# A hybrid decoder step on one Trainium2 core: the first stage reordered, seven up blocks on the first columns, four gates between the layers

## Chip, core and metric

One core of a Trainium2 chip runs the whole step as one launch. The metric is the device time of a launch in microseconds, as the median of several executions. One further execution is taken with the profiler, and its trace is what the rows below come from.

## The reference, cut to what matters

Two layers; 512 prompt rows and 8 sample rows (520 columns in the kernel) share the weights, D = 1024, all in float32.

```python
def block(x, ...):
    m, *states = mixer(rmsnorm(x, n_mix_pre), ...)
    x = x + rmsnorm(m, n_mix_post)
    f = square(relu(rmsnorm(x, n_ffn_pre) @ w_up)) @ w_down      # w_up 1024 x 4096
    return x + rmsnorm(f, n_ffn_post), *states

def mixer(xn, ...):
    rq, rk, rv, rg, hq, hf, hi, hgt, z, xbc, dt, gates = split(xn @ w_in)
    y_r = ...   # retention, 4 heads
    y_h = ...   # HGRN2, 8 heads: f from hf and a lower bound lb, q from hq, v from hi, gate hgt
    y_m = ...   # Mamba-2, 4 groups: conv on xbc, z, dt (16 columns), d_skip
    merged = sum over b of sigmoid(gates[b]) * (y[b] @ w_branch[b])
    return merged @ w_out, new states
```

## The kernel before, in words

**Blocks.** Activations lie transposed: 8 tiles of 128 channels by 520 columns. A projection block is 128 output channels. `mm3` (L210) makes it from three float32r products for each of 8 k-tiles (high weight by high activation, high by low, low by high), each on two column ranges, 0 to 256 and 256 to 520: 48 matmuls into one of two PSUM buffers (`pj`, L237). XN and YB are the two pairs of high and low activations. Called with `halves=(0,)` or `(1,)` it does one range only, 24 matmuls, a half block.

**Weights.** `wload` (L158) loads 512 KB into one of four raw buffers by SP and splits it on ACT (high part, L174) and DVE (low part, L175), four pieces each. The split parts go to two "w" buffers, to two sets of four general "u" tiles, or, for some, to parts of XN or YB. The list of uses is written out by hand from L1219 on; `weights` (L183) takes the next use and starts loads for up to AHEAD = 4 uses later, as long as their kind of buffer has one free.

**Order.** The program is traced in the order of the code, with `step()` moving generators ("tails") on by one yield after each block. A scheduler then orders each engine's queue by priority and its own time estimate: an instruction whose inputs it takes as ready may go earlier than traced. `keep_in_program_order` holds an instruction behind the one traced before it on its engine.

**First stage** (L1266 to 1308). SP loads x and the gain; one weight load is issued ahead (L1278). For five groups of rows ACT squares, DVE adds, POOL takes the power (L1286), DVE scales (L1290), PE transposes, ACT and DVE write XN (L1296, L1297). Then POOL loads the lower-bound logits (`lbr`) and eleven lists of rows in all (`vec_rows`, L376), SP the small ones of `params` (L407: dt_bias, a_log, d_skip, state_conv), the constants `cst` (1387 KB) and the masks. In layer 0 the first two blocks of head 0 are begun on the first columns.

**Between the layers.** The last down projection runs on the first columns, then on the second. `chain` (L335) for each range takes the mean square (`rstd`, L292: PE, DVE, POOL, DVE, PE, ACT), adds the residual, writes the next YB or XN without the norm's factor and at its end makes that factor, RR. Layer 1 begins (L1340 to 1353) with head 0's four blocks on YB's first columns, scaled by RR afterwards (`scaled`, L240). When the second range's chain is done, the tails `spill_x` and `normalized` (XN = norm of x, L368) are started, and head 0 does the second columns of its four blocks from the weights kept for it. Eight HGRN heads follow, each in eight steps; beside them `gate_ahead` (L1100) makes the 16 gates of branches 1 and 2 and stores them in DRAM. The 8 gates of branch 0 come late, after branch 2, into T1 (L1370).

**Up projection.** In the first group (`up_order`, L1199) NUP = 5 blocks run on the first columns while the chain of the second columns runs; then four of them from kept weights and the fifth from reloaded ones on the second; the other three on both. Their results (L1392) need RR.

## Time and profile before

| what | value |
|---|---|
| median of 3 runs | 2787.74 us (2787.11 to 2789.95) |
| the profiled execution, its own time | 2785.26 us |
| its span, first to last instruction | 2783.5 us |
| mean granted TensorE clock | 0.990 |
| PE busy, DVE, ACT, POOL | 98%, 61%, 42%, 26% of the span |

The span is what the rows below are measured in; their times start at its first instruction. Granted clock 1.00 is 2.4 GHz, 0.50 is 1.2 GHz. PE's matmuls are pipelined, so a matmul's own duration (some 283 ns) overlaps the next; the count in a window tells the rate.

### The profile page before, as it was taken

The page shows a single profiled execution, that of the slowest core. Times are in us where ns is not written, and L with a number is a line of the kernel's source. Part 1 is how long each engine was busy: PE and PEld are TensorE (multiplying, and loading weights), DVE is VectorE, ACT ScalarE, POOL GpSimd, SP SyncE. Part 2 cuts the span into 40 slices and gives each one's busy share as a digit, 9 for nine tenths or more (in the row PEclk, how much of TensorE's full clock was granted, in tenths as well). Part 3 has the DMA queues.
Part 4 walks back from the last instruction along what each step waited for, and adds up shares of the span by engine and source line. Part 5 has one row for each costly group of instructions (what it writes and reads, how often), then busy time and mean ns, then how long its engine had stood idle before and what let it go on. Part 6 is the DMA issues. An engine that isn't in the chain of part 4 may idle for free.

```text
span 2783.5 us, 56807 instructions
## 1 busy us (share of the span) xinstructions
PE 2720.9 (98%) x22489; PEld 2638.7 (95%) x22489; DVE 1690.8 (61%) x3714; ACT 1166.0 (42%) x2856; POOL 735.6 (26%) x939
## 2 busy tenths in 40 slices
PE   5999999999999999999989999999999999999999
PEld 5999999999999989999979999999999999899998
DVE  4575759986765553443576665799775645534443
ACT  3354545534333443332445444555253234533333
POOL 2353534341222031000144344434221310300004
PEclk8999999999999999999989999999999999999999
DMA  5544445573554413333324444456644534233331
GB/s 143 140 120 120 116 127 138 148 206 105 150 164 122 145 55 92 95 91 92 107 70 130 124 116 120 123 144 166 182 124 139 172 99 139 59 92 92 92 99 62
DMA packets 607578, 335.37 MB, mean 120 GB/s; under 512 B 96080, under 2 KB 581968, under 8 KB 607184
## 3 DMA queue, kind: packets, MB, share of 16 engines
q1 hardware_dynamic: 606672, 331.59, 42.4%
q8 instruction: 178, 2.92, 0.4%
q14 instruction: 88, 0.72, 0.1%
q0 software_dynamic: 640, 0.15, 0.0%
HBM read 287.61 MB, written 44.06 MB: 119 GB/s over the span
## 4 chain that ended last, share of the span: by engine, by line
PE 89%; DVE 4%; DMA 2%; issue 2%; ACT 2%; POOL 1%; SPq 1%; POOLq 0%; DVEq 0%; ACTq 0%
PE pj L215 78%; PE pm L290 3%; PE pm L506 1%; PE pm L466 1%; PE pm L514 1%; PE pm L882 1%; DVE w L175 1%; DMA wr<-in_w_in_dram 1%; ACT w L174 1%; DVE T L355 1%; PE pm L885 1%; PE pm L1049 0%; PE pm L1018 0%; DVE XL L360 0%; PE pm L633 0%
## 5 line engine op out<-in xcount | busy, mean ns | idle before, releaser
L215 PE MATMUL pj<-XH,w 128*128 128x256 f32 (+2 forms) x8896 | 1506.5, 286 | 7.7 <-ACT XH L282 3.5
L215 PEld LDWEIGHTS pj<-XH,w 128*128 128x128 f32 (+1 forms) x8896 | 1255.5, 188 | 30.7 <-issue 11.1
L174 ACT ACTIVATE w<-wr 128x256 fp32r<-128x256 f32 x1552 | 517.0, 404 | 1109.2 <-PE pj L215 980.3
L215 PE MATMUL pj<-XL,w 128*128 128x256 f32 (+2 forms) x4448 | 941.3, 286 | 5.4 <-DVE XL L360 3.3
L175 DVE TENSOR_TENSOR w<-wr,w 128x256 fp32r<-128x256 f32 x1552 | 651.8, 473 | 377.1 <-ACT w L174 376.8
L215 PEld LDWEIGHTS pj<-XL,w 128*128 128x128 f32 (+1 forms) x4448 | 703.7, 188 | 19.5 <-issue 10.7
L215 PE MATMUL pj<-YH,w 128*128 128x256 f32 (+1 forms) x3456 | 577.4, 285 | 5.3 <-DVE T L1120 2.3
L215 PEld LDWEIGHTS pj<-YH,w 128*128 128x128 f32 x3456 | 489.0, 189 | 11.7 <-ACT w L174 4.7
L215 PE MATMUL pj<-YL,w 128*128 128x256 f32 (+1 forms) x1728 | 366.0, 284 | 1.0 <-DVE YL L360 0.9
L215 PEld LDWEIGHTS pj<-YL,w 128*128 128x128 f32 x1728 | 275.9, 189 | 3.0 <-DVE YL L360 2.3
L320 POOL TENSOR_TENSOR u<-u,u 128x256 f32<-128x256 f32 (+1 forms) x56 | 47.3, 844 | 565.8 <-ACT u L319 565.8
L1392 DVE SCALAR_TENSOR_TENSOR u<-pj,RR 128x520 f32<-128x520 f32 (+2 forms) x74 | 46.1, 625 | 172.1 <-PE pj L215 169.9
L1409 POOL TENSOR_SCALAR T<-T,gn 128x256 f32<-128x256 f32 (+1 forms) x16 | 16.1, 1006 | 298.9 <-ACT u L316 298.9
L1404 DVE TENSOR_TENSOR T<-T,pj 128x520 f32<-128x520 f32 x32 | 22.3, 696 | 115.3 <-PE pj L215 115.3
L949 POOL TENSOR_TENSOR u<-u,cst 128x520 f32<-128x520 f32 x16 | 22.1, 1380 | 201.3 <-ACT u L948 191.3
L290 PE MATMUL pm<-ident,u 128*128 128x128 f32 (+3 forms) x320 | 49.7, 276 | 20.5 <-DVE u L1290 20.4
L628 POOL TENSOR_TENSOR u<-u,s 128x512 f32<-128x512 f32 x32 | 39.1, 1240 | 86.2 <-DMA u<-in_state_hgrn_dram 73.5
L290 PEld LDWEIGHTS pm<-ident,u 128*128 128x128 f32 (+3 forms) x320 | 37.3, 145 | 22.6 <-DVE u L1290 10.9
L290 PE MATMUL pm<-ident,T 128*128 128x128 f32 (+1 forms) x368 | 56.3, 282 | 1.3 <-DVE u L1164 1.0
L1122 POOL TENSOR_TENSOR T<-T,u 128x520 f32<-128x520 f32 x16 | 29.1, 1822 | 99.8 <-DVE u L1120 99.8
L754 POOL TENSOR_TENSOR u<-u,u 128x544 f32<-128x544 f32 x32 | 45.9, 1434 | 34.8 <-DVE u L753 34.8
L863 POOL COPY s<-u 128x4 f32<-128x4 f32 x32 | 17.3, 543 | 142.1 <-ACT u L861 142.1
(319 smaller groups left out, 3346.3 us busy)
## 6 DMA issues: line engine op xcount, KB each, us to landing
wr<-in_w_in_dram SPq DMA_DIRECT2D x208, 512.0 KB
wr<-in_w_up_dram SPq DMA_DIRECT2D x66, 512.0 KB
wr<-in_w_down_dram SPq DMA_DIRECT2D x64, 512.0 KB
u<-rbd SPq DMA_DIRECT2D x96, 256.0 KB
wr<-in_w_branch_dram SPq DMA_DIRECT2D x48, 512.0 KB
out_dram<-u SPq DMA_DIRECT2D x72, 256.0 KB
out_dram<-u SPq DMA_DIRECT2D x72, 128.0 KB
gate<-u SPq DMA_DIRECT2D x32, 260.0 KB
```

The source lines that it names most:

```text
L174: a = S.activation(out=hi, in_=rq, func=AF.Copy)
L175: b = V.tensor_tensor(out=lo, in0=rq, in1=hi.bitcast(F32), op=ALU.subtract)
L215: PE.matmul(ps[:m, CH[h]], lhsT=wt(k), rhs=act[:, k, CH[h]], start=st, stop=sp_)
L290: PE.transpose(out, in_, ident[:k, :k])
L320: (eng or V).tensor_tensor(out=acc, in0=acc, in1=sq, op=ALU.add)
L355: V.tensor_tensor(out=x, in0=x, in1=t, op=ALU.add)
L466: PE.matmul(po[32 * c:32 * c + 32, :2 * width], lhsT=qz[:, c, :], rhs=st[:, off:off + 2 * width], start=True, stop=True, tile_position=(0, ...
L506: PE.matmul(pl[:, cs[c]], lhsT=w[:, cs[c]], rhs=u[:, cs[c]], start=True, stop=True)
L628: G.tensor_tensor(out=c3(sts[i]), in0=c3(sts[i]), in1=bc(fs[:, s0, None], shc), op=ALU.mult)
L754: G.tensor_tensor(out=c, in0=c, in1=e, op=ALU.add)
L1122: G.tensor_tensor(out=T2[:, d, :], in0=T2[:, d, :], in1=dst, op=ALU.add)
L1392: V.scalar_tensor_tensor(out=a, in0=ps[:, c], scalar=0.0, in1=RR[:, c], op0=ALU.max, op1=ALU.mult)
```

## The change

- First stage: the logits' and layer 0's row loads on POOL come ahead of the x loads. Two weight loads are placed after the second and third group of rows, with their splits in traced order. The constants are loaded in two parts, the larger one (K_COS to K_RK, up to K_TRI) only after head 3 of layer 0; dt_bias, a_log, d_skip and state_conv are loaded after head 1 of layer 0 and used after head 3, in layer 1's case after the third and the fourth MLP group of layer 0. d_skip comes as one contiguous broadcast of 16 numbers, and POOL copies out of it.
- The 16-column dt weights: load and split are held in traced order; their block runs on columns 0 to 512 and 512 to 520.
- NUP is 7: seven up blocks on the first columns, then 3 to 6 from kept weights and 0 to 2 from reloaded ones on the second, then block 7 on both.
- Layer 1: after head 0's four first-column blocks, four gates of branch 0 (d = 0 to 3) on the first columns; after the chain the same four on the second, from kept weights, with tanh and a store to DRAM. Head 0's weights are loaded a second time. Late in layer 1 only gates 4 to 7 are left; the branch reads the other four from DRAM. The gates beside the heads are two for each head in both layers.

```diff
@@ -47,7 +47,8 @@
 AHEAD = 4
-NUP = 5
+NUP = 7
+NEG = 4
@@ -152,13 +153,18 @@
 
+    def pin(ins):
+        tc.keep_in_program_order(ins)
+
...
         raw = wp.tile([P, NB, n], F32, tag=f"raw{n}", name=nm("wr"), bufs=4 if n == 128 else 1)
-        SY.dma_start(out=raw, in_=src.rearrange("(k p) m -> p k m", p=P))
+        dma = SY.dma_start(out=raw, in_=src.rearrange("(k p) m -> p k m", p=P))
+        if n != 128:
+            pin(dma)
@@ -173,19 +179,25 @@
             b = V.tensor_tensor(out=lo, in0=rq, in1=hi.bitcast(F32), op=ALU.subtract)
-            if key in pinned:
-                tc.keep_in_program_order(a)
-                tc.keep_in_program_order(b)
+            if key in pinned or n != 128:
+                pin(a)
+                pin(b)
...
 
-    def weights(src, ahead=False):
+    def preload():
+        key = order.pop(0)
+        live[key_info[key][2]] += 1
+        pinned.add(key)
+        wload(key)
+
+    def weights(src):
...
         key = uses[i]
-        assert ahead or key[0] == str(src), i
+        assert key[0] == str(src), i
         for j in list(order):
-            if first[j] > i + (0 if ahead else AHEAD):
+            if first[j] > i + AHEAD:
@@ -195,24 +207,20 @@
             order.remove(j)
-            if ahead:
+            with tc.high_priority(WOFF):
                 wload(j)
-            else:
-                with tc.high_priority(WOFF):
-                    wload(j)
-        if ahead:
-            return
...
 
-    def mm3(ps, w, ah, al, halves=(0, 1), m=P, ks=range(NB)):
+    def mm3(ps, w, ah, al, halves=(0, 1), m=P, ks=range(NB), cuts=None):
...
                 for h in halves:
-                    PE.matmul(ps[:m, CH[h]], lhsT=wt(k), rhs=act[:, k, CH[h]], start=st, stop=sp_)
+                    c = (cuts or CH)[h]
+                    PE.matmul(ps[:m, c], lhsT=wt(k), rhs=act[:, k, c], start=st, stop=sp_)
@@ -248,13 +256,18 @@
             return ps
-        ps = pj()
         if (l, c0) in early:
+            ps = pj()
...
             return raw
-        mm3(ps, weights(w_cols(l, c0, n)), *XN, m=n)
+        if n != P:
+            ps = psj.tile([P, 1024], F32, tag="pj", name=nm("pj"))[:, :T]
+            mm3(ps, weights(w_cols(l, c0, n)), *XN, m=n, cuts=(slice(0, SEQ), slice(SEQ, T)))
+            return ps
+        ps = pj()
+        mm3(ps, weights(w_cols(l, c0, n)), *XN)
@@ -412,18 +425,6 @@
             vec_rows(rb, 8 * i, a[l])
-        sc = pp.tile([16, 4], F32, tag="sc", name=nm("sc"))
-        SY.dma_start(out=sc[:, 0:1], in_=dt_bias[l].rearrange("(h o) -> h o", o=1))
-        SY.dma_start(out=sc[:, 1:2], in_=a_log[l].rearrange("(h o) -> h o", o=1))
-        dk = pp.tile([P, 8], F32, tag="dk", name=nm("dk"))
-        dv = d_skip[l].rearrange("(b two) -> two b", two=2)
-        for q in range(2):
-            SY.dma_start(out=dk[64 * q:64 * q + 64, :], in_=dv[q:q + 1, :].to_broadcast([64, 8]))
-        rcs = []
-        for hf in range(4):
-            rc = ut()[:24, :512]
-            SY.dma_start(out=rc, in_=state_conv[l].rearrange("s r c -> (s r) c")[:, 512 * hf:512 * hf + 512])
-            rcs.append(rc)
@@ -442,8 +443,24 @@
         p["lb"] = lbp
+        yield
+        sc = pp.tile([16, 4], F32, tag="sc", name=nm("sc"))
+        pin(SY.dma_start(out=sc[:, 0:1], in_=dt_bias[l].rearrange("(h o) -> h o", o=1)))
+        pin(SY.dma_start(out=sc[:, 1:2], in_=a_log[l].rearrange("(h o) -> h o", o=1)))
+        dk = pp.tile([P, 8], F32, tag="dk", name=nm("dk"))
+        dv = sp.tile([P, 16], F32, tag="dv", name=nm("dv"), bufs=1)
+        pin(SY.dma_start(out=dv, in_=d_skip[l:l + 1, :].to_broadcast([P, 16])))
+        rcs = []
+        for hf in range(4):
+            rc = ut()[:24, :512]
+            pin(SY.dma_start(out=rc, in_=state_conv[l].rearrange("s r c -> (s r) c")[:, 512 * hf:512 * hf + 512]))
+            rcs.append(rc)
+        yield
...
         p["sc"] = sc
+        for q in range(2):
+            x = slice(64 * q, 64 * q + 64)
+            G.tensor_copy(out=dk[x, :], in_=dv[x, :].rearrange("p (b two) -> p b two", two=2)[:, :, q])
@@ -1093,15 +1110,24 @@
     def gates_at(l, h, i):
-        at = {0: (3,), 1: (0, 1, 3)}.get(h, (1, 3)) if l else (1, 3)
-        n = 2 * h - (l > 0 and h == 1)
-        return [(1 + g // NB, g % NB) for g in (n + k for k, x in enumerate(at) if x == i)]
+        return [(1 + g // NB, g % NB) for g in (2 * h + i // 2,) if i % 2]
+
+    early_gates = [(0, d) for d in range(NEG)]
+
+    def late_from(l):
+        return NEG if l else 0
+
+    def g_col(b, d):
+        return C_GATE + 1024 * b + 128 * d
...
     def gate_ahead(l, b, d):
-        ps = proj(l, C_GATE + 1024 * b + 128 * d)
+        ps = proj(l, g_col(b, d))
...
         S.activation(out=t, in_=ps, func=AF.Tanh, scale=0.5)
-        gates[l, b, d] = kept = dp.tile([P, T], F32, tag="gate", name=nm("gate"), bufs=2 * NB)
+        keep_gate(l, b, d, t)
+
+    def keep_gate(l, b, d, t):
+        gates[l, b, d] = kept = dp.tile([P, T], F32, tag="gate", name=nm("gate"), bufs=2 * NB + NEG)
@@ -1109,7 +1135,7 @@
         for d in range(NB):
-            if mode == "last":
+            if mode == "last" and d >= late_from(l):
@@ -1218,8 +1244,15 @@
         held = {}
-        for i, c in enumerate(early_cols if l else early_cols[:2]):
-            held[c] = add(w_cols(l, c), store="wu"[i % 2] if l else "w")
+        if l:
+            for i, c in enumerate(early_cols):
+                add(w_cols(l, c), store="wu"[i % 2])
+            gheld = [add(w_cols(l, g_col(*g)), store="wu"[i % 2]) for i, g in enumerate(early_gates)]
+            for key in gheld:
+                use(key)
+        else:
+            for c in early_cols[:2]:
+                held[c] = add(w_cols(l, c))
@@ -1239,7 +1272,7 @@
             add(w_br(l, 2, d))
-        for d in range(NB):
+        for d in range(late_from(l), NB):
@@ -1265,6 +1298,11 @@
     xts = [[t[:, :512], t[:, 512:]] for t in xts] + [xs_]
+    lbr = sp.tile([P, P], F32, tag="prow", name="lbr", bufs=3)
+    for j in range(depth):
+        vec_rows(lbr, 8 * j, hg_lb_logits[j])
+    loading = params(0, prms[0])
+    next(loading)
@@ -1274,7 +1312,6 @@
         SY.dma_start(out=xs_[i], in_=rows[4][0][:, 512 * i:512 * i + 512])
-    weights(None, True)
@@ -1295,17 +1332,14 @@
             V.tensor_tensor(out=lo, in0=c3(ps)[:, :, :n], in1=hi.bitcast(F32), op=ALU.subtract)
-    lbr = sp.tile([P, P], F32, tag="prow", name="lbr", bufs=3)
-    for j in range(depth):
-        vec_rows(lbr, 8 * j, hg_lb_logits[j])
-    loading = params(0, prms[0])
-    next(loading)
-    SY.dma_start(out=cst, in_=cst_in)
+        if c in (1, 2):
+            preload()
+    pin(SY.dma_start(out=cst[:, K_TRI:], in_=cst_in[:, K_TRI:]))
     mskf = uw(384)
-    SY.dma_start(out=mskf, in_=msk_in)
+    pin(SY.dma_start(out=mskf, in_=msk_in))
...
     lba = lower_bounds(lbr)
-    next(loading, None)
+    next(loading)
@@ -1338,17 +1372,23 @@
         else:
-            spare = [T2[:, i, :] for i in (0, 2, 7, 1)]
-            for i, c in enumerate(early_cols):
-                raw = spare[i]
+            spare = [T2[:, i, :] for i in (0, 2, 7, 1, 3, 4, 5, 6)]
+            for raw, c in zip(spare, early_cols + [g_col(*g) for g in early_gates]):
...
                 scaled(raw, ps, 0)
-                early[(l, c)] = raw
                 step()
+            early.update(((l, c), raw) for c, raw in zip(early_cols, spare))
...
             tails.append(normalized(XN, p["mpre"]))
+            for raw, g in zip(spare[len(early_cols):], early_gates):
+                ps = pj()
+                mm3(ps, weights(w_cols(l, g_col(*g))), *YB, halves=(1,))
+                scaled(raw, ps, 1)
+                S.activation(out=raw, in_=raw, func=AF.Tanh, scale=0.5)
+                keep_gate(l, *g, raw)
+                step()
@@ -1356,6 +1396,11 @@
                 G.memset(RR, 0.0)
+            if l == 0 and h == 1:
+                next(loading)
+            if l == 0 and h == 3:
+                next(loading, None)
+                pin(SY.dma_start(out=cst[:, :K_TRI], in_=cst_in[:, :K_TRI]))
@@ -1367,7 +1412,7 @@
             split((YB[0][:, d, :], YB[1][:, d, :]), T1[:, d, :])
-        for d in range(NB):
+        for d in range(late_from(l), NB):
@@ -1419,6 +1464,9 @@
             if gi == 2 and l + 1 < depth:
+                next(loading)
+                next(loading)
+            if gi == 3 and l + 1 < depth:
```

## Rows read from the trace of the kernel before

**Rows 1.** The page, parts 1 and 2: PE's total; granted clock in 40 slices, in tenths.
```profile
PE 2720.9 (98%) x22489; PEld 2638.7 (95%) x22489; DVE 1690.8 (61%) x3714; ACT 1166.0 (42%) x2856; POOL 735.6 (26%) x939
...
PEclk8999999999999999999989999999999999999999
```

**Rows 2.** Windows of 20 us: stretch, length, busy us (instructions) of each engine, clock, DMA.
```profile
1020.00:1040.00 20.00, 17.94 (x146) 16.68 (x144) 14.44 (x22) 8.95 (x21) 8.76 (x9) 1.00 0.10 28
1040.00:1060.00 20.00, 17.53 (x125) 16.57 (x124) 6.67 (x19) 8.33 (x23) 6.74 (x10) 0.83 0.26 77
1240.00:1260.00 20.00, 20.00 (x169) 20.00 (x168) 10.61 (x24) 9.53 (x23) 0.00 (x0) 1.00 0.28 80
1400.00:1420.00 20.00, 18.15 (x139) 16.48 (x138) 14.27 (x31) 5.75 (x15) 5.73 (x6) 0.92 0.33 107
1420.00:1440.00 20.00, 15.10 (x96) 13.75 (x94) 15.18 (x30) 11.52 (x23) 9.72 (x14) 0.82 0.23 80
1440.00:1460.00 20.00, 16.53 (x129) 15.85 (x130) 16.23 (x25) 7.37 (x15) 13.39 (x13) 0.83 0.21 54
...
2400.00:2420.00 20.00, 16.41 (x110) 14.69 (x109) 12.64 (x22) 9.44 (x23) 8.92 (x9) 0.84 0.09 27
```
The five busy columns are PE, PEld (weight load), DVE, ACT and POOL; then granted clock, DMA share, GB/s.

**Rows 3.** Waits of PE, whole span: us in total, times, longest.
```profile
PE pm L290 <- DVE u L1290: 20.4, 3, 9.9
```

**Rows 4.** The chain that ended last, first 60 us: start, us, what.
```profile
16.92 16.28 DMA wr<-in_w_in_dram
...
46.84 6.46 PE pj L215 x34
```

**Rows 5.** Windows of 2 us in the first stage, columns as in rows 2.
```profile
20.00:22.00 2.00, 2.00 (x16) 2.00 (x15) 1.96 (x4) 1.74 (x6) 0.47 (x1) 1.00 0.05 0
...
46.00:48.00 2.00, 1.41 (x6) 1.40 (x7) 0.76 (x5) 0.22 (x1) 1.47 (x3) 0.50 1.03 186
```

**Rows 6.** Timeline of the first stage: start, us, instruction, idle before and its end.
```profile
7.09 0.55 POOL L1286 TENSOR_TENSOR s<-s,nhalf 128x1 f32<-128x1 f32 x1 [5.38 <-DVE s L1285]
...
22.57 0.14 DVE L1284 TENSOR_TENSOR s<-s 8x1 f32<-8x1 f32 x1
...
33.18 11.08 SPq L161 DMA_DIRECT2D wr<-in_w_in_dram  x3
33.22 0.59 ACT L174 ACTIVATE w<-wr 128x32 fp32r<-128x32 f32 x4 [11.15 <-DMA wr<-in_w_in_dram]
...
33.59 0.13 DVE L1285 TENSOR_SCALAR s<-s 8x1 f32<-8x1 f32 x1
...
34.29 1.30 POOL L378 DMA_DIRECT2D lbr<-in_hg_lb_logits_dram  x2
...
36.41 0.81 PE L215 MATMUL pj<-XH,w 128*128 128x264 f32 x2
...
46.53 0.52 POOL L378 DMA_DIRECT2D rb<-in_norm_mix_post_dram  x1 [7.82 <-DMA lbr<-in_hg_lb_logits_dram]
```

**Rows 7.** DMA issues, first 80 us: line, engine, count, KB, us from issue to landing.
```profile
lbr<-in_hg_lb_logits_dram POOLq DMA_DIRECT2D x2, 4.0 KB, 11.7
...
rb<-in_norm_mix_post_dram POOLq DMA_DIRECT2D x1, 4.0 KB, 3.9
```

**Rows 8.** Timeline between the layers: the second range's mean square, 16 matmuls of 2 columns.
```profile
1425.59 1.07 PE L298 MATMUL pm<-ones,u 128*66 128x2 f32 x16
```

**Rows 9.** The page, part 5: the weight splits, busy us, mean ns, idle before.
```profile
L174 ACT ACTIVATE w<-wr 128x256 fp32r<-128x256 f32 x1552 | 517.0, 404 | 1109.2 <-PE pj L215 980.3
...
L175 DVE TENSOR_TENSOR w<-wr,w 128x256 fp32r<-128x256 f32 x1552 | 651.8, 473 | 377.1 <-ACT w L174 376.8
```

**Rows 10.** Instructions by line, 990 to 1060 us: ns min/median/max, first and last start, forms.
```profile
L1392 DVE SCALAR_TENSOR_TENSOR u<-pj,RR x10: 409/424/433, 1018.2 to 1055.2; 128x256 f32<-128x256 f32 x5, 128x264 f32<-128x264 f32 x5
...
L360 DVE SCALAR_TENSOR_TENSOR XL<-T,gn,XH x10: 471/490/1324, 1010.5 to 1038.2; 128x264 fp32r<-128x264 f32 x8, 128x256 fp32r<-128x256 f32 x2
...
L283 POOL TENSOR_TENSOR YL<-u,YH x10: 727/753/907, 1020.9 to 1057.3; 128x256 fp32r<-128x256 f32 x5, 128x264 fp32r<-128x264 f32 x5
```

## The prediction, made before the changed kernel was built

> **What bounds the kernel now.** I read the page's totals first. The reader should see that TensorE (PE) is busy 98% of the span and that its granted clock leaves full speed in only a few of the 40 slices [rows 1]. So the kernel is PE-bound nearly everywhere, and a change that adds no PE work can gain only where PE stands or runs at its lower level.
>
> The table of windows says how much. A dense 20 us window holds 169 matmuls, 0.118 us each, so a half block of 24 matmuls is worth 2.84 us. The three windows of the gap between the layers hold 139, 96 and 129 matmuls instead of 507: 143 are missing, 16.9 us. The two windows around the second pass of the first up group hold 146 and 125 in layer 0 (67 missing, 7.9 us), and 110 in layer 1's worst one (59 missing, 7.0 us) [rows 2]. In these windows the granted clock averages 0.82 to 0.92: PE fell from 2.4 to 1.2 GHz after it had stood for lack of input.
>
> The first stage is the biggest hole. In the list of PE's waits its transposes stand 20.4 us for the normalized rows (L1290) [rows 3]. The chain of waits then names what follows, 16.28 us for a weight load, and at its end 34 matmuls that take 6.46 us, 0.19 us each [rows 4], because the granted clock is at 0.50 by then [rows 5]. They end at 53.30 us. The timeline shows the mechanism. At 22.57 us VectorE (DVE) adds the sums of the last rows. Its next instruction is a split of a 128x32 piece of the 16-column dt weights, which waits for ScalarE (ACT), which waits 11.15 us for the DMA; the sample rows go on only at 33.59 and the second half's first matmul comes at 36.41. PE then meets the transpose of the lower-bound logits, which POOL issued only at 34.29 us, and stands until 46.6, when POOL too is released [rows 6]. The SP queue shows why loads land late: the weight issues from 33.18 on take 11.08 us, right behind the second pair of d_skip loads, and in a 2 us window behind the first pair the DMA engines are 0.05 busy and move nothing [rows 5, 6].
>
> **The change part by part.** The profiled execution took 2785.26 us (span 2783.5); the median of the runs shown, 2787.74, is 2.48 above it. I make the sum against the first and add 2.48.
>
> *First stage.* Three things go: the early dt split, the logits behind the row work, and the element-by-element d_skip load. After 22.57 the sample rows need the 2.82 us that [rows 6] show from 33.59 to 36.41, so the second half could begin at 25.5. What is late next is POOL: the eleven row loads are now pinned ahead of its first power, which ran at 7.09. Eleven issues at 0.52 to 0.65 us end near 7.5, and the ninth waits for the first to land, as it did before (7.82 us) [rows 6]. Landing took 11.7 us behind the d_skip loads and 3.9 us for the last three [rows 7]; I take a value near the 3.9, since nothing clogs the queue now. That delays the first 128 rows by 0 to 2.5 us, partly hidden under the second; I put 1 us and start at 26.5. The 36 matmuls that had been done at 53.30 then need 36 x 0.118 = 4.2 us, and the state of 53.30 is reached at 30.7: 22.6 us gained. The bounds are 24 (no delay) and 11 (one of the two waits stays). The weights of the next blocks were landing in 26 to 50 us before; now the DMA has no silence, so I charge nothing. If that cover is gone, each late load holds PE for about a half block, 2.8 us.
>
> *Small loads moved.* dt_bias, a_log, d_skip, state_conv and the large part of the constants are issued on SP later, in traced order, some behind stores that wait for compute. Weight loads queue behind them, but four raw buffers hold 20 us of PE work. Two POOL copies per layer and the transposes of the conv state move, not grow. The dt weights are split in traced order, so ACT may stand for their landing again; PE has two PSUM blocks, 11.4 us, before it notices. I charge 1 us in all, with 0 to 5 per layer as bounds.
>
> *dt block.* 48 matmuls of 256 and 264 columns become 24 of 512 and 24 of 8. The trace has none of 8; 16 of 2 columns took 1.07 us, 0.07 each [rows 8]. With 24 x 0.22 (estimated as just under twice 0.118) + 24 x 0.07 = 6.9 against 5.7, I charge 1.2 us per layer, 2.4 in all; bounds 0 and 2 per layer.
>
> *Seven up blocks.* Two more half blocks (5.7 us) run before PE needs the second half of XN, and two weights more are loaded per layer. A load costs ACT 4 x 0.33 and DVE 4 x 0.42 = 1.68 us [rows 9]. So DVE gets two splits and two evictions at 0.42, 4.2 us, in the stretch in which it also runs the chain whose end (RR of the second half) releases PE by way of the evictions (L1392) [rows 10]. DVE was busy 14.44 of the 20 us from 1020 [rows 2], so I let half of the 4.2 delay the chain: 5.7 - 2.1 = 3.6 us per layer, 7.2 in all. Bounds are 0 and 5.7 each.
>
> Here a second row speaks against the change: a split of the chain (L360) takes 0.49 us in the median but up to 1.32 [rows 10]; in the timeline the slow ones lie beside POOL's additions (L363). Two more of POOL's subtractions (L283), 0.75 us each, come into this stretch. If each holds DVE for its length, 1.5 us per layer go too. The Trainium skill (GPSIMD Engine Reference, Key points) says the same in general: GpSimd shares its SBUF interfaces with VectorE and contends with its two-input instructions. By that rule the gain would be 2.1 instead of 3.6 per layer.
>
> *Four gates between the layers.* Eight half blocks, 22.7 us of PE work, move from late in layer 1, where PE is dense, into the gap. The layer's later gates lose half their blocks; the remaining four, 22.7 us, still cover the 8 splits of YB before the first branch. New on SP are four stores and four reloads of 260 KB, and four weight loads more, because head 0's weights are no longer kept. DVE, busy 45.7 of the 60 us, gets 8 splits (13.4 us) and 8 evictions (3.4 us): 62.5 us. PE then has 364 x 0.118 + 22.7 = 65.7 us of dense work where it took 60 + 22.7. If nothing stands the gain is 16.9. If DVE keeps the share of its busiest window, 0.81, the stretch takes 77 us and the gain is 5.6. PE also has to live through the RR chain that begins at 1425.59 with two PSUM buffers, and the eight steps of normalizing XN (L325) now run under gates that don't need XN [rows 8]. I take 10, between the ends; the range goes from 3 to 16.9.
>
> Sum: 22.6 + 7.2 + 10 - 2.4 - 1 = 36.4, so 2748.9 profiled and **2751** for the median.
>
> **Rivals.**
> *DVE becomes the bound in the up stretch and in the gap.* For it: its share there and the stretched L360; against it: its free 5.6 us from 1020 on. The up blocks then bring nothing and the gap 4: 22.6 + 4 - 3.4 = 23, so 2765. The Trainium skill's sharing of SBUF interfaces (GPSIMD Engine Reference, Key points) would point this way.
> *Only one of the two waits of the first stage goes,* because POOL's row loads still hold the powers, or a load still lands late. The start brings 11: 2787.7 - (11 + 17.2 - 3.4) = 2763. Against it: the silence of the DMA queue follows the d_skip loads both times.
> *Everything fits:* 24 + 11.4 + 16.9 - 1 = 51, so 2736. Against it: both stretches have a chain that ends in a PE, POOL, DVE, PE, ACT sequence which no block removes.
> *Slower: the dt split.* Place: before head 5, in both layers. ACT stands in order for the 64 KB of 64-byte runs, DVE behind it, and PE once its two buffers are full. The load took 16.28 us on the chain [rows 4], of which some 5 would show per layer. It decides the sign only from a landing of about 32 us, when it costs 21 per layer: 36 gained, 42 lost, 2793. The landing lay behind a silent queue before, which speaks against it.
> *The change does not do what it says:* the scheduler still orders by its own estimate, and the pin holds an instruction only behind its predecessor. That would look like the second rival, and is counted there.
>
> **How the numbers follow.** Forecast 0.53, DVE-bound 0.22, one start wait left 0.08, everything fits 0.12, slower 0.03, and 0.02 for a sum of mishaps that lands on no change. Within 0.2% (5.6 us, about what a measurement of this kernel can tell from none) lies only that last case. The forecast's own range, from the bounds of the three gains taken together, is 2742 to 2760. Taking in the two cases near 2764 and leaving out most of 2736, the range is 2738 to 2768.
>
> **What would show it.** Right: the sample rows' first 264-column matmul near 26 us and the first dense window from about 28; no dt split before 100 us; no silent DMA windows in the first 50 us; matmul counts in the up windows up by some 30 per layer and in the gap's windows above 130 each; four gates with line numbers of the new early loop. Wrong: POOL waiting behind its ninth row load past 12 us; DVE at 19 of 20 us in the gap with PE waiting on it; ACT idle for over 10 us before a 128x32 split; PE waits in the steady stretches that hold none now.

## The result and the profile after

The changed kernel takes **2758.89 us** in the median (2757.0 to 2760.38) against 2787.43 for the kernel before on the same chip: a ratio of 0.9897, interval 0.9882 to 0.9913, so 28.5 us less. The forecast was 2751 with a range of 2738 to 2768: faster as forecast, inside the range, 8 us short of the size. The profiled execution took 2760.38 us (span 2758.4) against 2785.26 (span 2783.5), 24.9 less; the ledger below is made on these two. That is 3.6 us under the difference of the medians, since the profiled execution of the changed kernel is the slowest of its four and that of the kernel before lies under its median.

The page, parts 1 and 2, answers to [rows 1]: PE does the same 22489 matmuls in 12 us less busy time, and no slice's clock lies under nine tenths now.

```profile
PE 2709.0 (98%) x22489; PEld 2625.5 (95%) x22489; DVE 1699.1 (62%) x3754; ACT 1177.2 (43%) x2896; POOL 746.9 (27%) x951
...
PEclk9999999999999999999999999999999999999999
```

The table of 20 us windows answers to [rows 2], with the same columns. The three windows of the gap hold 447 matmuls where they held 364, at full clock. The second window of the up group holds 154 in both layers, where the worst of before held 125 and 110.

```profile
1000.00:1020.00 20.00, 18.19 (x143) 17.47 (x143) 14.11 (x33) 10.91 (x30) 7.42 (x8) 0.95 0.44 125
1020.00:1040.00 20.00, 18.55 (x154) 18.26 (x154) 13.30 (x25) 10.57 (x28) 9.33 (x10) 0.96 0.10 27
1400.00:1420.00 20.00, 17.22 (x143) 16.23 (x142) 15.27 (x33) 7.59 (x20) 4.97 (x4) 1.00 0.48 146
1420.00:1440.00 20.00, 17.43 (x139) 16.88 (x139) 18.73 (x39) 15.03 (x29) 1.32 (x2) 1.00 0.48 141
1440.00:1460.00 20.00, 18.71 (x165) 18.15 (x164) 15.55 (x32) 11.62 (x29) 14.22 (x23) 1.00 0.50 138
...
2380.00:2400.00 20.00, 18.29 (x154) 17.70 (x155) 15.28 (x28) 10.98 (x29) 10.52 (x10) 1.00 0.19 53
```

The list of PE's waits answers to [rows 3]. The wait for the normalized rows fell from 20.4 to 12.8 us; 12.0 of it is the wait for the first rows at the start of the run. The second line is new: PE waits for ScalarE's weight split, twice for over 3 us.

```profile
PE pm L303 <- DVE u L1327: 12.8, 3, 12.0
PE pj L223 <- ACT w L180: 8.5, 4, 3.4
PE pj L223 <- DVE T L249: 3.9, 4, 1.3
PE pj L223 <- DVE u L1437: 3.6, 2, 1.8
```

The timeline of the first stage answers to [rows 6]. POOL's ninth row load waits 2.10 us for the first to land, and the first power runs at 10.57 us (7.09 before). The second column range's matmuls, which began at 36.41, begin at 27.86 and are dense from 29.40.

```profile
7.89 0.52 POOL L391 DMA_DIRECT2D rb<-in_norm_mix_post_dram  x1 [2.10 <-DMA lbr<-in_hg_lb_logits_dram]
...
10.57 0.61 POOL L1323 TENSOR_TENSOR s<-s,nhalf 128x1 f32<-128x1 f32 x1
...
27.86 0.52 PE L223 MATMUL pj<-XH,w 128*128 128x264 f32 x2
...
29.40 0.39 PE L223 MATMUL pj<-XL,w 128*128 128x264 f32 x1 [0.76 <-DVE XL L1334]
```

**The ledger.** Start times of the same instruction in both traces give the lead of a run: how many us earlier than in the kernel before it starts. Heads are the HGRN heads, counted from 0 and taken at one ACT instruction of each (L519 before, L536 now); the dt block lies between heads 4 and 5. Below it stand the leads of the runs of the next section.

```
event (its time before)            changed  x1    x2    x9    x3    x10   x8    x11   x7
head 2, layer 0 (140.1)              20.4  19.9  21.2  20.3  19.9  20.5  17.4  22.6  20.1
head 4, layer 0 (228.0)              19.1  18.6  19.9  19.1  18.7  19.2  16.1  21.4  18.8
head 5, layer 0 (279.4)              12.4  17.1  15.0  17.8  13.0  17.9  15.1  20.3  13.3
first up group begins (968.8)        12.4  17.0  15.1  18.2  13.4  18.0  15.2  20.3  13.4
up group is over (1171.0)            16.0  20.6  18.6  21.3  13.7  16.5  18.6  24.9  16.9
end of layer 0 (1401.4)              17.2  21.8  19.8  22.6  14.9  17.8  19.9  26.2  18.1
head 2, layer 1 (1512.2)              3.6   8.5   6.3   9.3   1.7   4.5   6.3  12.9  15.3
head 7, layer 1 (1739.1)             -2.1   6.2   1.0   8.0  -3.9   2.2   4.9  11.6   9.3
first up group begins (2341.1)       20.7  29.3  23.7  30.6  18.5  25.8  27.3  34.4   9.6
up group is over (2544.4)            25.8  33.7  28.7  34.6  17.2  25.1  32.7  38.9  12.9
end (2780.1)                         25.1  33.1  28.1  34.0  17.2  25.1  32.2  38.3  12.3
```

The first stage gains 20.4, the up groups 3.6 and 5.1, the gap 17.2 to 3.6 and later, when the moved gates are missing, -2.1 to 20.7: -13.6 + 22.8 = 9.2. Against them stand **6.7 and 5.7 us lost at the dt block**, in layer 0 and layer 1.

### The profile page after: what moved, and what is told of

It reads as the page before. It is cut to its first block, busy times and chain, and to the rows that moved or that the text cites. A ratio compares the mean times of both kernels' runs of the same rounds, so it can differ in the third digit from the quotient of the medians.

```text
span 2758.4 us, 56964 instructions
## 1 busy us (share of the span) xinstructions
PE 2709.0 (98%) x22489; PEld 2625.5 (95%) x22489; DVE 1699.1 (62%) x3754; ACT 1177.2 (43%) x2896; POOL 746.9 (27%) x951
## 5 line engine op out<-in xcount | busy, mean ns | idle before, releaser
L223 PE MATMUL pj<-XH,w 128*128 128x256 f32 (+2 forms) x8768 | 1485.9, 286 | 13.3 <-ACT w L180 7.7
L223 PEld LDWEIGHTS pj<-XH,w 128*128 128x128 f32 (+1 forms) x8768 | 1235.8, 188 | 38.6 <-ACT w L180 15.9
L180 ACT ACTIVATE w<-wr 128x256 fp32r<-128x256 f32 x1584 | 528.1, 404 | 1064.6 <-PE pj L223 962.2
L223 PE MATMUL pj<-XL,w 128*128 128x264 f32 (+2 forms) x4384 | 931.4, 286 | 0.8 <-DVE XL L1334 0.8
L181 DVE TENSOR_TENSOR w<-wr,w 128x256 fp32r<-128x256 f32 x1584 | 665.5, 473 | 370.4 <-ACT w L180 369.2
L223 PEld LDWEIGHTS pj<-XL,w 128*128 128x128 f32 (+1 forms) x4384 | 693.8, 188 | 14.6 <-issue 11.3
L223 PE MATMUL pj<-YH,w 128*128 128x256 f32 (+1 forms) x3584 | 597.7, 284 | 8.2 <-DVE T L249 3.9
L223 PEld LDWEIGHTS pj<-YH,w 128*128 128x128 f32 x3584 | 505.8, 188 | 15.2 <-ACT w L180 5.7
L223 PE MATMUL pj<-YL,w 128*128 128x256 f32 (+1 forms) x1792 | 381.4, 283 | 0.9 <-DVE YL L373 0.9
L223 PEld LDWEIGHTS pj<-YL,w 128*128 128x128 f32 x1792 | 286.0, 188 | 1.5 <-DVE YL L373 1.1
L303 PE MATMUL pm<-ident,u 128*128 128x128 f32 (+3 forms) x320 | 49.1, 275 | 12.8 <-DVE u L1327 12.8
L1438 ACT ACTIVATE u<-u 128x520 f32<-128x520 f32 (+2 forms) x78 | 42.8, 549 | 33.0 <-DVE u L1437 33.0
```

Source lines behind the costliest of these rows:

```text
L180: a = S.activation(out=hi, in_=rq, func=AF.Copy)
L181: b = V.tensor_tensor(out=lo, in0=rq, in1=hi.bitcast(F32), op=ALU.subtract)
L223: PE.matmul(ps[:m, c], lhsT=wt(k), rhs=act[:, k, c], start=st, stop=sp_)
L303: PE.transpose(out, in_, ident[:k, :k])
L1438: S.activation(out=t, in_=a, func=AF.Square)
```

## The experiments

x2 to x7 have one execution each. Those of the kernel before range from 2783.53 to 2791.05 us in all its runs on record, so the weight of x2 to x7 lies in the ledger more than in their time.

### The dt block: the load, or the cut

The timeline of the changed kernel around the dt block of layer 0 shows a queue, not a slow load. SP issues nothing between 239.14 and 247.77 us: the next instruction on it is a gate's store, whose tile is only then computed. The dt load stands behind it, as one of the two issues at 248.16, and has landed 2.7 us later; ACT waits 2.20 us for it, PE 3.39.

```profile
238.77 0.37 SPq L165 DMA_DIRECT2D wr<-in_w_in_dram  x1
...
247.77 0.34 SPq L1131 DMA_DIRECT2D gate<-u  x1
248.16 1.18 SPq L165 DMA_DIRECT2D wr<-in_w_in_dram  x2
...
250.83 0.59 ACT L180 ACTIVATE w<-wr 128x32 fp32r<-128x32 f32 x4 [2.20 <-DMA wr<-in_w_in_dram]
...
251.11 0.61 PE L223 MATMUL pj<-XH,w 128*16 128x512 f32 x2 [3.39 <-ACT w L180]
```

The same stretch in windows of 4 us (columns as in [rows 2]) shows the second half of the price: behind the wait the granted clock is 0.50, PE's lower level of 1.2 GHz, for a whole window.

```profile
248.00:252.00 4.00, 0.89 (x4) 0.33 (x5) 1.64 (x7) 1.22 (x6) 0.00 (x0) 0.75 0.86 199
252.00:256.00 4.00, 4.00 (x20) 3.93 (x19) 0.57 (x1) 0.00 (x0) 1.64 (x2) 0.50 0.42 150
256.00:260.00 4.00, 4.00 (x30) 1.79 (x29) 0.94 (x1) 0.00 (x0) 0.40 (x1) 0.90 0.01 2
```

**x1_dt_early** issues this load one head earlier.

```diff
+            if h == HDT - 1:
+                key = next(k for k in order if key_info[k][1] == 16)
+                order.remove(key)
+                wload(key)
             if h == HDT:
                 unit(ssd_dt(l, p, dtp), 1)
```

> Changed kernel, with the load and split of the 16-column dt weights traced at the start of head 4 instead of four blocks ahead of their use. Theory (late issue): in the changed kernel the load is issued at 248.2 us, behind a gate's store that waits for compute, PE stands 3.4 us for its split and the block then runs at half clock; with the load ahead the wait is 0 and the clock stays full, and from head 4 to head 5 the lead over the kernel before falls by under 2 us instead of 8.0 (layer 0) and 5.7 (layer 1). So 10 to 12 us faster than the changed kernel, 2747 to 2750. Rival (the cut into 512 and 8 columns is what costs): the loss stays at 5 us or more per layer, under 4 us faster.

Measured: 2751.7 us (2750.46 to 2752.72), ratio 0.9872 (0.9856 to 0.9889). Between heads 4 and 5 the lead falls by 1.5 us instead of 6.7. In layer 1, from head 2 to head 7, it falls by 2.3 instead of 5.7. In its list of PE's waits the line for the split falls from 8.5 to 1.8 us, and neither of the two that are left (17.62 and 1402.47 us) stands at a dt block:

```profile
PE pj L223 <- ACT w L180: 1.8, 2, 1.0
```

So the late issue is the cause of 8.6 of the 12.4 us; the gain of 7.2 in the time is below the 10 to 12 that were expected.

**x2_dt_cuts** leaves the load where the change has it, and undoes the cut.

```diff
-        if n != P:
-            ...
         ps = pj()
-        mm3(ps, weights(w_cols(l, c0, n)), *XN)
+        mm3(ps, weights(w_cols(l, c0, n)), *XN, m=n)
```

> Changed kernel, the dt block alone cut as before (256 and 264 columns, the usual PSUM buffer); load and split still late. Theory (late issue): the wait of 3.4 us for the split stays; the block is 0.5 to 1.5 us shorter per layer, 2757 to 2760. Rival (the cut costs): 5 us per layer come back, about 2749.

Measured: 2758.66 us, the time of the changed kernel. The lead still falls by 4.9 us at head 5 and by 5.3 in layer 1, and in the list of PE's waits the line for the split stays:

```profile
PE pj L223 <- ACT w L180: 8.4, 4, 3.3
```

With the old cut 10.2 of the 12.4 us are still lost, so the cut accounts for 2.2 at most. **x9_early_cut** has both edits.

> The changed kernel with the early issue of the dt weights in both layers (as in x1_dt_early) and the old cut of the dt block (24 matmuls of 256 and 24 of 264 columns), nothing else. Theory: with the load early, the 512 + 8 cut costs what its matmuls cost, 1.2 to 1.5 us per layer, so the old cut gives 2.4 to 3.0 us in all below x1_dt_early (2751.7): 2748 to 2750, with head 5 losing about 0.3 us per layer in the ledger of events instead of 1.5 and 1.9. Rival: the old cut shows the same loss, because the rest of the loss is not the block's matmuls but ScalarE's and VectorE's four splits of its weights or the turn between PSUM buffers; then 2751 to 2753 and a loss of 1.0 to 1.4 per layer, as in x8_all_three.

Measured: 2751.06 us (2749.1 to 2751.57), ratio 0.987 (0.9855 to 0.9884). It loses 1.3 us in each layer where x1 loses 1.5 and 2.3. What the cut costs beside an early load is then 0.2 and 1.0 us, under the charge of 1.2; in the time it can't be told from nothing, since 2751.06 lies among the runs of x1. The rival expectation was the better one. Most of the 1.3 in layer 0 (0.87 us) and half of it in layer 1 (0.67) is waiting in head 4, behind the early split, for steps of the head itself on ACT (L637) and DVE (L577). The changed kernel has no wait there.

```profile
221.36 1.16 PE L646 MATMUL pm<-u,u 128*128 128x128 f32 x8 [0.44 <-ACT u L637]
...
223.19 0.48 PE L223 MATMUL pj<-XH,w 128*128 128x256 f32 x2 [0.43 <-DVE T L577]
...
1604.90 0.48 PE L223 MATMUL pj<-XH,w 128*128 128x256 f32 x2 [0.67 <-DVE T L577]
```

### The up blocks: five, seven, eight

**x3_nup5** is the changed kernel with five blocks, as before the change.

```diff
-NUP = 7
+NUP = 5
```

> Changed kernel with five up blocks on the first columns instead of seven. Theory (as predicted, 3.6 us per layer, measured from one event to another 3.5 and 5.1): 8 to 9 us slower than the changed kernel, 2767 to 2769, and PE's matmul count around the second pass falls by about 30 in layer 0. Rival (the lead came from elsewhere, such as the order of the queues): under 4 us slower.

Measured: 2767.84 us, 8.95 above the changed kernel. The lead grows by 0.3 us in the first up group and falls by 1.3 in the second, where the changed kernel gains 3.6 and 5.1. From 1000 to 1040 us PE runs 270 matmuls, 27 fewer than the changed kernel, as expected. So the two blocks are worth 3.3 and 6.4 us, 9.7 in all, and nothing else in the change touches this stretch much.

**x10_early_nup8** is x1_dt_early with `NUP = 8`.

> x1_dt_early with eight up blocks on the first columns instead of seven. Theory (each half block run before the second half of the rows is ready fills 2.84 us of a hole, less what its split and eviction put on VectorE): the first up group gained 3.5 and 5.1 us from two blocks more, so what is left of the hole decides. The missing matmuls of the changed kernel's two windows are 169 - 143 = 26 and 15 in layer 0, 11 and 15 in layer 1, 4.8 and 3.1 us with the clock's part in it; one half block more gives at most half of this: 1 to 2 us per layer, 2 to 4 in all, so 2748 to 2750. Rival: VectorE binds the stretch and the eighth block adds its 2.1 us of split and eviction to the chain: no gain or a loss of up to 1 us per layer, 2751 to 2754.

Measured: 2761.66 us (2761.08 to 2762.3), ratio 0.9909 (0.9894 to 0.9924): 10 us **slower** than x1. The theory fell, and the rival's sign was right, but at five times its size: the lead changes by -1.5 and -0.7 us in the two groups, against +3.6 and +4.4 in x1, so the eighth block costs 5.1 us per layer. In the windows of 10 us of x10 VectorE is busy 9.68 of 10 us while PE stands, and the clock is 0.83 in the two windows behind it.

```profile
1010.00:1020.00 10.00, 5.90 (x48) 5.72 (x48) 9.68 (x18) 6.30 (x16) 5.22 (x4) 1.00 0.37 105
1020.00:1030.00 10.00, 8.37 (x64) 8.28 (x64) 4.63 (x9) 3.02 (x7) 4.36 (x4) 0.83 0.19 54
1030.00:1040.00 10.00, 9.60 (x65) 9.53 (x65) 3.42 (x10) 4.84 (x15) 2.22 (x3) 0.83 0.11 33
```

In its list of PE's waits the evictions (L1441 here) come to 7.9 us, against 3.6 in the changed kernel, and the timeline has the longest of them. Between PE's last matmul, at 1017.03, and the eviction that it waits for, at 1019.76, VectorE runs three weight splits (L181) and two steps of the chain (L373). Later PE also stands 1.81 us for the chain's mean square (L318), 1.45 in x1.

```profile
1016.97 1.73 DVE L181 TENSOR_TENSOR w<-wr,w 128x256 fp32r<-128x256 f32 x2
1018.62 0.89 DVE L373 SCALAR_TENSOR_TENSOR XL<-T,gn,XH 128x264 fp32r<-128x264 f32 x2
...
1019.76 0.41 DVE L1441 SCALAR_TENSOR_TENSOR u<-pj,RR 128x256 f32<-128x256 f32 x1
...
1020.23 0.39 PE L223 MATMUL pj<-XH,w 128*128 128x256 f32 x1 [2.92 <-DVE u L1441]
```

In x1 the same window has VectorE at 9.79 as well, and PE stands in it once, for 1.79 us:

```profile
1010.00:1020.00 10.00, 8.21 (x57) 8.04 (x56) 9.79 (x19) 6.74 (x17) 5.97 (x5) 0.83 0.37 105
```

So VectorE is full there with seven blocks too, and its share alone does not tell seven from eight; what the eighth adds is a second stand. From 990 to 1045 us PE's waits come to 7.0 us in x10 and 3.8 in x1, and one more window at 0.83 is worth some 1.7 us (an estimate, 10 x 0.17): 4.9 of the 5.1 lost in layer 0. That the eighth block's own split and eviction cause the second stand fits VectorE's order, and was not tried apart.

### The first stage: which edit carries it

Here the three things that go are put one at a time into the kernel *before*, whose lead is 0 by definition.

**x4_dskip**: only the d_skip load, as one contiguous row per partition.

```diff
-        for q in range(2):
-            SY.dma_start(out=dk[64 * q:64 * q + 64, :], in_=dv[q:q + 1, :].to_broadcast([64, 8]))
+        SY.dma_start(out=dv, in_=d_skip[l:l + 1, :].to_broadcast([P, 16]))
...
+            G.tensor_copy(out=dk[x, :], in_=dv[x, :].rearrange("p (b two) -> p b two", two=2)[:, :, q])
```

> Kernel before with one part of the first stage alone: d_skip loaded as one contiguous broadcast of 16 numbers, with two POOL copies. Theory (the element-by-element d_skip loads silence the DMA queue for 8 to 10 us each): the two silences go, the dt load that landed at 33.2 us lands some 9 us earlier, the logits land 4 to 6 us after their issue instead of 11.7, and the first head is 14 to 18 us earlier than in the kernel before: 2769 to 2773. Rival (the silence belongs to the dt load's or dt_bias' short runs): the waits of 11 and 9 us stay and the time is within 3 us of before.

Measured: 2771.7 us, as expected, with a lead of 16.0 us at head 2 and 13.7 at the end. In 2 us windows the DMA moves 333 GB/s where [rows 5] show nothing:

```profile
20.00:22.00 2.00, 2.00 (x16) 2.00 (x15) 2.00 (x4) 1.81 (x5) 0.36 (x1) 1.00 0.98 333
22.00:24.00 2.00, 2.00 (x20) 2.00 (x19) 0.52 (x2) 0.20 (x2) 0.00 (x0) 1.00 0.60 93
```

The logits land 4.3 us after their issue instead of 11.7 [rows 7], and ACT waits 1.9 us for the dt weights instead of 11.15 [rows 6]. The element-wise load alone carries 16.0 of the changed kernel's 20.4.

**x5_rows_first**: only the row loads and the logits ahead of the row work.

```diff
+    lbr = sp.tile([P, P], F32, tag="prow", name="lbr", bufs=3)
+    for j in range(depth):
+        vec_rows(lbr, 8 * j, hg_lb_logits[j])
+    loading = params(0, prms[0])
+    next(loading)
     for c in range(3):
         SY.dma_start(out=T1f...
```

> Kernel before with one part of the first stage alone: the POOL row loads (logits and layer 0's lists) ahead of the x loads; d_skip and the dt split as before. Theory (the dt split's wait and the logits' are separate, one behind the other, and both go back to the d_skip loads): the wait of 9.4 us for the logits goes, the 10 us wait for the dt split stays, the first pow is some 3 us later as in the changed kernel; the first head 9 to 12 us earlier, 2776 to 2779. Rival (the logits' position is what held the first stage): 18 us or more.

Measured: 2793.46 us, some 6 us slower than before: a miss. The lead is -4.7 at head 2. The wait for the logits is gone, but PE's waits only change their names: the rows again, and a load that stands behind the second d_skip pair on SP.

```profile
PE pm L290 <- DVE u L1296: 19.1, 2, 16.6
PE pj L215 <- ACT XH L1302: 7.3, 1, 7.3
PE pm L290 <- DMA u<-in_state_conv_dram: 6.3, 1, 6.3
```

In the first line 16.6 us are the wait for the first rows, which PE has at 16.65 us and had at 8.49 in the kernel before; that is more than the lead lost. The first power is done by 11.4 us, but ACT and DVE have a weight's split queued ahead of scaling those rows, and it waits for its load:

```profile
14.05 1.34 ACT L174 ACTIVATE w<-wr 128x256 fp32r<-128x256 f32 x4 [7.89 <-DMA wr<-in_w_in_dram]
14.50 1.43 DVE L175 TENSOR_TENSOR w<-wr,w 128x256 fp32r<-128x256 f32 x4 [7.96 <-ACT w L174]
```

So this run mixes two things, and does not show what the rows' place alone is worth. In a window of 4 us the DMA is as silent as it was:

```profile
20.00:24.00 4.00, 2.74 (x12) 2.43 (x13) 3.23 (x7) 2.28 (x7) 0.96 (x2) 1.00 0.04 0
```

**x6_dt_pin**: only the dt weights' load and split held in traced order.

```diff
-            if key in pinned:
+            if key in pinned or n != 128:
```

> Kernel before with the dt weights' load and split held in traced order, nothing else. Theory: the 11 us wait of ACT at 22 us goes, but the logits are issued by POOL at some 24 us and still land behind a silent queue, and the dt block before head 5 now waits and runs at half clock: the first head 6 to 12 us earlier, minus some 5 us at head 5 in each layer; 2784 to 2791, no faster than 0.2%. Rival (only the dt split held the first stage): first head 20 us earlier, 2777 or less.

Measured: 2790.27 us, inside the expected range and not told apart from the kernel before. The lead is 4.3 at head 2, where 6 to 12 had been expected, then -0.8 behind the dt block of layer 0 and -5.9 behind that of layer 1; -5.0 at the end. By itself the pin loses more at the two dt blocks (5.1 and 3.4 us) than it brings at the start. PE's list of waits has both kinds of the line: the rows, and the split.

```profile
PE pj L217 <- ACT XH L1298: 9.4, 1, 9.4
PE pj L217 <- ACT w L176: 6.7, 2, 3.4
```

### POOL's row loads ahead of the first power

Two runs move row loads behind a power, on top of x9's edits. **x8_all_three** moves the nine of the layer's parameters behind the first group's power; **x11_rows_split** moves the last three behind the second group's.

```diff
+            if i == 4:
+                yield
             vec_rows(rb, 8 * i, a[l])
...
         G.tensor_tensor(out=rs[:n, :], in0=rs[:n, :], in1=nhalf[:n, :], op=ALU.pow)
+        if c == 1:
+            next(loading)
```

This is x11's edit; x8's has `c == 0` and no split of the rows.

> Changed kernel with three edits: the dt load one head earlier, the dt block cut at 256 as before, and layer 0's row loads on POOL behind the first group's power (only the logits' two ahead). Theory: the dt loss goes to under 1 us per layer (early load: minus 1.5 to 1.9 left, all of it the cut), and the first power, now at 10.6 us, comes back to 7 to 8 us, which brings the first stage forward by 2 to 3 us: 2 x 1.6 + 2.5 = 5.7 us below the 2751.7 of the early load alone, 2744 to 2748. Rivals: the cut was neutral (then 2749), or the first stage is held by DVE and not by the power (then 2748 to 2749).

> x9_early_cut with POOL's last three row loads (the 9th to the 11th) issued behind the second group's power, where POOL stood for 2.86 us, instead of ahead of the first power. Theory (the ninth outstanding row load waits for the first one's landing, and this alone held the first power to 10.57 us): the first power runs at 7.1, the second no later than 12.97, and the lead of the changed first stage rises from 19.9 to 21.2 by 1 to 2.5 us; time 2746 to 2749. Rival: the first stage is paced by VectorE and ScalarE on the later rows, where the wait was hidden: lead within 0.7 us of x9_early_cut and the same time. As x8_all_three showed, row loads that hold a later power cost instead: if the three hold the third power beyond 16.4 us, the lead falls.

x8 measured 2755.05 us (2753.31 to 2755.34), ratio 0.9885 (0.9868 to 0.9901), a miss. POOL's timeline shows why: the first power is back at 7.08, but the nine loads, and among them the wait for an early one's landing, now stand ahead of the second.

```profile
7.08 0.58 POOL L1317 TENSOR_TENSOR s<-s,nhalf 128x1 f32<-128x1 f32 x1 [3.89 <-DVE s L1316]
...
13.65 0.52 POOL L387 DMA_DIRECT2D rb<-in_norm_ffn_post_dram  x1 [1.82 <-DMA ra<-in_conv_w_dram]
14.19 0.59 POOL L1317 TENSOR_TENSOR s<-s,nhalf 128x1 f32<-128x1 f32 x1
...
26.64 0.54 POOL L1317 TENSOR_TENSOR s<-s,nhalf 8x1 f32<-8x1 f32 x1 [6.02 <-DVE s L1316]
```

The sample rows' power comes at 26.64 us, 1.86 later than in the changed kernel (24.78), and the lead at head 2 falls to 17.4. At the two dt blocks x8 loses 1.0 and 1.4 us, where under 1 was expected. In x11 every power is earlier and the three loads fit where POOL stood:

```profile
6.87 0.58 POOL L1321 TENSOR_TENSOR s<-s,nhalf 128x1 f32<-128x1 f32 x1 [0.53 <-DVE s L1320]
11.29 0.56 POOL L1321 TENSOR_TENSOR s<-s,nhalf 128x1 f32<-128x1 f32 x1 [3.85 <-DVE s L1320]
...
12.89 0.52 POOL L387 DMA_DIRECT2D rb<-in_norm_ffn_post_dram  x1
...
23.10 0.54 POOL L1321 TENSOR_TENSOR s<-s,nhalf 8x1 f32<-8x1 f32 x1 [3.07 <-DVE s L1320]
```

Its lead at head 2 is 22.6 us, 2.3 above x9's. The time is 2750.14 us (2747.28 to 2753.76), ratio 0.9872 (0.9855 to 0.9888): just above the 2746 to 2749 that were expected. The profiled execution was its fastest, and its runs spread over 6.5 us, so that it is not told apart from x9 or x1. The theory's mechanism is shown at the start; whether the 2.3 us reach the end of the run stays open.

### The gates between the layers

**x7_no_gates** is the changed kernel with the gap as before: head 0's weights kept, no early gates, and the late gates at their old places.

```diff
-NEG = 4
+NEG = 0
...
-                add(w_cols(l, c), store="wu"[i % 2])
-            gheld = [add(w_cols(l, g_col(*g)), store="wu"[i % 2]) for i, g in enumerate(early_gates)]
-            for key in gheld:
-                use(key)
+                held[c] = add(w_cols(l, c), store="wu"[i % 2])
```

> Changed kernel with the gap between the layers undone: head 0's four blocks kept from the first pass, no gates of branch 0 there, the 16 other gates placed as before, 8 late gates. Theory (the moved gates give PE work while DVE and ACT finish the chain and the norm, 9.5 us by the events): 8 to 11 us slower than the changed kernel, 2767 to 2770. Rival (DVE bound; the gates bring nothing): within 3 us.

Measured: 2774.6 us, 15.7 above the changed kernel, more than either theory expected; the ledger shows 12.8 of it. Its lead goes from 18.1 to 15.3 over the gap and the late part gives 0.3, -2.5 in all against the changed kernel's +9.2: the gates are worth 11.7 us. The second up group brings 3.3 instead of 5.1. The first two windows of the gap are as thin as in [rows 2], and below full clock:

```profile
1400.00:1420.00 20.00, 15.52 (x85) 12.91 (x84) 14.19 (x27) 10.45 (x20) 7.25 (x8) 0.74 0.29 107
1420.00:1440.00 20.00, 14.81 (x106) 14.36 (x105) 17.27 (x30) 8.71 (x18) 15.54 (x19) 0.83 0.20 53
```

Why the gap without gates is 2.5 us worse than in the kernel before was not tried.

## Why the prediction was right, and where it was not

```
term                    forecast   measured   off by
first stage                22.6       20.4     -2.2
seven up blocks             7.2        8.7     +1.5
four gates in the gap      10.0        9.2     -0.8
dt block and its load      -2.4      -12.4    -10.0
small loads moved          -1.0       -0.8     +0.2
sum                        36.4       25.1
```

The last line but one is what is left of the ledger: -1.3 at head 4 of layer 0, where the conv state's transposes stand now, 1.2 at the end of layer 0 and -0.7 after the last up group. The spans differ by 25.1 us, the executions by 24.9.

**The step that failed** is the landing of the dt weights, priced inside the term of the small loads at 1 us in all, with 0 to 5 per layer as bounds, because "PE has two PSUM blocks, 11.4 us, before it notices". With the cut's part it was put at 3.4 and measured 12.4. The two blocks were no cover: they hold results that PE has written, not work to come. PE stands from 247.72 us (251.11 less 3.39), before the load is even issued at 248.16. The bounds did hold it: 6.7 and 5.7 lie under the 5 + 2 per layer that stood for wait and cut. The place of the slower rival was right, before head 5 in both layers, and its mechanism was not: it made ACT stand for a slow landing of 64-byte runs, but the load lands within 2.7 us. It is issued late, since SP stands behind a gate's store. The text had named that queue ("some behind stores that wait for compute"), and covered it with "four raw buffers hold 20 us of PE work"; for a load of 16 columns, used one block later, that cover does not exist. x1 shows the cause of 8.6 of the 12.4 us, and x2 leaves 2.2 at most to the cut.

**First stage.** The mechanism was right in the main: the dt split and the logits are off the path, and so is the load that had silenced the DMA. One of the signs named for it did not come, since there still is a silent window. From 32 to 36 us the DMA moves nothing. But SP issues nothing between 25.49 and 35.12 us, and PE is busy all through the window, so it is not the hole of before:

```profile
24.92 0.57 SPq L1339 DMA_DIRECT2D u<-in_msk_dram  x1
35.12 6.64 SPq L165 DMA_DIRECT2D wr<-in_w_in_dram  x2
```

```profile
32.00:36.00 4.00, 4.00 (x37) 4.00 (x36) 2.94 (x12) 2.77 (x6) 0.00 (x0) 1.00 0.00 0
```

The gain is 2.2 us short. POOL's hold of the first power was put at 0 to 2.5 us, with 1 taken; the power came 3.48 us late (10.57 for 7.09), since the row load that the ninth waits for, for 2.10 us, took 6.2 us to land and not some 3.9. x11 takes this hold away and leads by 22.6, 2.3 more than x9, so the hold cost 2.3 where 1 was charged. That is 1.3 of the 2.2; the rest stays open. The second range's first matmul, put at 26.5, comes at 27.86. Which of the three edits mattered had been left open, and x4 to x6 answer it for one: the d_skip load, with 16.0 us. Without it the pin brings 4.3 at head 2 and loses more at the dt blocks, and x5 does not tell the rows' worth. The placing of the two early weight loads was not tried by itself.

**Up blocks.** 3.6 and 5.1 against 3.6 each. The Trainium skill's sharing rule (GPSIMD Engine Reference, Key points), by which 2.1 was left, is not borne out here as a loss of that size; whatever the slow splits beside POOL cost, it did not add up to that on the path. The prediction gave its windows a clock of 0.82 to 0.92; its own row for 1020 to 1040 us has 1.00 [rows 2], so there PE stood without slowing down. But the rival "DVE becomes the bound" was only one block away: x10.

**Gap.** 9.2 against 10, in the lower half of 3 to 16.9. VectorE is busy 18.73 of 20 us in its second window, close to the 19 that had been named as a sign of being wrong, and PE waits 3.9 us in all for its evictions (L249). So "everything fits" fails on VectorE's share; the chain that the prediction set against it holds PE for 0.7 us in the gap (L318).

**The numbers.** 2758.89 lies in the range and, with 1.1 us to spare, in the forecast's own (2742 to 2760). Two of its four runs lie above that. The mechanism of the forecast came about in all three gains. On the profiled executions the sum is 11.3 us short, 10.0 of it in the dt term; on the medians it is 7.9. That the up blocks' 1.5 too much stands against 2.2 and 0.8 too little elsewhere is luck.

## What to carry to other kernels

When a load is held in traced order, look at what stands ahead of it on its queue, and not only at how long it takes: here a 64 KB load stood behind a store that waited for compute, and issuing it one head earlier gave back 8.6 of 12.4 us. Free PSUM buffers did not cover late weights. And filler has an end: two blocks more brought 9.7 us in two layers, with VectorE already at 9.79 of 10 us in one window (x1), and the eighth cost 5.1 in each. A full window on the other engine says that the end is near, not which block passes it.

## What was not expected of the hardware

A load of 2 KB in 4-byte pieces held up the loads behind it: with it, the window from 20 to 22 us moves nothing [rows 5], and the three weight issues behind it take 11.08 us [rows 6], 2.78 in x4; read as a 64-byte row per partition, 8 KB in all, it leaves 333 GB/s in that window, and the kernel is 16 us ahead after the first stage. The Trainium skill (DMA: Bandwidth & Descriptors, Why small descriptors are slow) says that small pieces carry a fixed overhead each; the runs agree in direction, and show that it reaches other queues' loads (the logits on POOL's: 11.7 against 4.3 us). A long issue alone is no sign of it: in the changed kernel three weight issues from 14.29 us take 10.58 us, with 281 GB/s moving from 16 to 20 us.

A stand cost PE half as much again and more: the clock was at 0.50 for a whole window of 4 us behind it, and 6.7 us were lost for 3.39 waited in the changed kernel, 4.9 for 3.31 with the old cut (x2). By an estimate from the windows the clock makes up the difference: 0.75, 0.50 and 0.90 from 248 to 260 us miss 3.4 us of full speed in the changed kernel, and 0.85, 0.72 and 1.00 miss 1.7 in x2.
